# Mamba input tiles of a hybrid decoder step: handed to the scan by blocks, with three fixed tiles

## The chip, the cores and the metric

The kernel runs on one core of a Trainium2 chip. A core has TensorE (PE, matrix products), VectorE (DVE), ScalarE (ACT), GpSimd (POOL) and DMA queues, here driven by SyncE (SP); each works off its own instructions in their written order and waits for the others by semaphores. The metric is the device time of one execution in microseconds, as the median of several runs.

## The reference

One step of a trunk with two layers, for a prompt of 1024 tokens and eight samples of one token each. Layer 0 is a Conformer convolution module, layer 1 a Mamba-2 mixer; each is followed by a SwiGLU network and a small gated embedding. All is float32. The change lies in the Mamba mixer:

```python
zxbcdt = u @ w_in                                   # z 2048, x 2048, B 1024, C 1024, dt 32 columns
xbc, new_conv = causal_dwconv(xbc, conv_buf, w_conv, b_conv)     # 4 taps over the tokens
xbc = jax.nn.silu(xbc)
...
y, final = ssd(xs, dt, A, Bm, Cm, s0)               # 8 groups; 8 chunks of 128 tokens in each
y = y + d_skip * xs
yg = y * jax.nn.silu(z)
yg = yg * lax.rsqrt(jnp.mean(yg * yg, axis=-1, keepdims=True) + EPS)   # within a group
out = (yg * norm_g) @ w_out
```

In `ssd` a chunk's output is the sum of a product within the chunk (`y_diag`: C times B, weighted by decays, times x) and one with the state that the chunks before it left; then the state is decayed and the chunk's own contribution added. The samples take one step of the same recurrence, each from a state of its own.

## The kernel before

Activations are stored with channels on the 128 partitions and tokens along the row. A row has T = 1032 columns, eight phases of 128 prompt tokens and one sample each. Every float32 product is made of three (`mm3`, L130 to L132) of a rounded part `hi` and a rest `lo` of each factor; ScalarE makes `hi` (L110), VectorE `lo` (L111).

**Input tiles.** `in_proj` computes one tile of 128 columns of `u @ w_in`. It goes through the tokens in three blocks (BLKP) of 388, 386 and 258 columns, 24 matmuls each, into one of three PSUM banks with the tag `mm`; `by_token` lets ScalarE evict the bank, in two or three pieces (L843, L848), into the tile in the order of tokens. After a block `tick` counts down the queued transposes (`later`), so that two blocks later the matmul stream takes them up. A generator, `in_proj` yields after each block.

**Raw tiles.** The eviction of an x, B or C tile goes to a raw tile with three zero columns ahead of the tokens for the convolution. `new_raw` takes it from a pool with two places and clears the three columns by a memset on POOL (L815). `xbc_tile` calls it, drives `in_proj` to its end, and then issues the convolution for both halves of the tokens: a product on ScalarE (L980), three multiply-adds on VectorE (L983), silu on ScalarE (L985). Thus a place is free again when its convolution has been done. `z_tile` does the same for z, without a convolution. `to_tokens` transposes a half into tokens by rows (L1005 on TensorE, L1006 on ScalarE).

**Scan.** The order of the input tiles is a list: B, C, x, x, z, z of a group, then the same of the next. The loop over 64 chunks (8 groups of 8) issues in each turn: the decays and the C times B product of the next chunk (`weights_a`), in some turns one whole input tile of the next group, and the chunk's own work (`scale_x`, `chunk`). In a group these turns are those of chunks 0, 1, 3, 4, 5 and 7:

```python
STEPS = (0, 1, 3, 4, 5, 7)
...
elif cc in STEPS:
    step()
```

In `chunk` TensorE makes `ys` (L1093, C with the state before), four `yd` (L1097, within the chunk) and the chunk's contribution to the state (L1109). VectorE makes `yo` (L1102), `yv` (L1099, L1105), `ztok` (L1106) and `state` (L1114 decays it, L1117 adds); ScalarE squares (L1107). After chunk 1 comes `sample`, the samples' step for this group, in four parts: POOL makes two products (L1159, L1160), VectorE an addition (L1161), a product (L1163) and a sum (L1164). The samples' B and C (`bcs`, L1148) go out to memory and come back to all partitions as `bcb` (L1152), a single tile for two of the parts. Where matmuls of one engine stand between others' it is the scheduler's placing; the order on VectorE, ScalarE and POOL is made before the run too.

In group 7 there is no next group: its turns are filled with the first two quarters of the w_out product, whose inputs are loaded into tiles of the same pool (`staging`).

Of the kernel before, what the change touches and what calls it, by code (L numbers as in the profile page):

```python
# [8 lines left out]
F32 = mybir.dt.float32  # L9
F32R = mybir.dt.float32r  # L10
AF = mybir.ActivationFunctionType
# [5 lines left out]
P = 128  # L17
# [4 lines left out]
T = SEQ + NS  # L22
# [35 lines left out]
def trunk_kernel(ctx: ExitStack, tc: tile.TileContext, I, O):  # L58
    nc = tc.nc
    V, S, G, TE = nc.vector, nc.scalar, nc.gpsimd, nc.tensor  # L60
# [85 lines left out]
    def later(k, fn):  # L146
        queue.append([k, fn])
# [83 lines left out]
    def ple_products(pool, ps, i, pt, tag, halves=(0, 1), w=None):  # L231
        for s in halves:
            w = w or kview(slab(I["w_proj"][i, s], 1024), 2)
            for mm in range(4):
                m = 4 * s + mm
                stg = pool.tile([P, T], F32, name="pstg", tag=tag, bufs=3 if tag == "v" else 2)
                for o, n in BLK:
                    a = ps.tile([P, 512], F32, name="a", tag="mm")
                    product(a[:, :n], w, mm * P, pt, o, n)
                    S.activation(out=stg[:, o:o + n], in_=a[:, :n], func=AF.Copy)  # L240
                nc.scalar.dma_start(out=proj_d[i][m], in_=stg)
                yield
            w = None
# [295 lines left out]
    with tc.tile_pool(name="l0", bufs=2, reuse_waits="tile") as pool:  # L539
# [50 lines left out]
        with tc.tile_pool(name="conv", bufs=2, reuse_waits="tile") as cp:  # L590
# [93 lines left out]
            it = pw1(0, vs, w1)  # L684
# [18 lines left out]
            for m in range(KT):  # L703
# [4 lines left out]
                if m == KT - 1:  # L708
# [4 lines left out]
                    it = chain(ple_products(cp, ps, 1, U[6:], "v"), ple_products(cp, ps, 0, U[4:6], "v", (1,)))  # L713
# [52 lines left out]
            for m in range(KT):  # L766
                x, y, z = apply(0, m)
# [6 lines left out]
            for b in (1, 2):  # L774
                finish(b, (y,), (z,))
                for m in range(KT):
                    x, y, z = apply(b, m)
# [4 lines left out]
    for j in range(2):  # L782
# [4 lines left out]
        for m in range(KT):  # L787
            w = kview(slab(I["w_pw2"][m], 1024), KT)
# [21 lines left out]

    l1 = ExitStack()
    pa = l1.enter_context(tc.tile_pool(name="l1a", bufs=1, reuse_waits="tile"))
    def new_raw():
        raw = pa.tile([P, 3 + T], F32, name="raw", tag="raw", bufs=2)
        G.memset(raw[:, 0:3], 0.0)  # L815
        return raw

    raws = [new_raw(), new_raw()]
    cst = pa.tile([P, 32, NS, 4], F32, name="cst")
    ncp = pa.tile([P, 32, 3], F32, name="ncp")  # L820
    xs_all = pa.tile([P, 32, NS], F32, name="xs_all")
    zs_all = pa.tile([P, 16, NS], F32, name="zs_all")
# [28 lines left out]
    def in_proj(w, dst, sample, func, off=0):  # L851
        for o, n in BLKP:
            a = bank("mm", mm_bufs[0])
            product(a[:, :n], w, 0, U, o, n)
            by_token(dst[:, off:off + T], a, o, n, func)
            if o == BLKP[-1][0]:
                G.tensor_copy(out=sample, in_=dst[:, off + SEQ:off + T])
            tick()
            yield
# [16 lines left out]
    with tc.tile_pool(name="ps1", bufs=1, space=PSUM, reuse_waits="tile") as ps, \  # L876
            tc.tile_pool(name="l1b", bufs=2, reuse_waits="tile") as pool:
        mm_bufs[0] = 3
        C9 = 9
        nac = pool.tile([P, 8, NH], F32, name="nac", bufs=1)  # L880
        ea = pool.tile([P, 8, NH], F32, name="ea", bufs=1)
        dtd = pool.tile([P, 8, NH], F32, name="dtd", bufs=1)
# [11 lines left out]
        def decays():  # L894
# [3 lines left out]
            def v9(t, i):  # L898
                return t[:, 288 * i:288 * i + 288].rearrange("p (c h) -> p c h", c=C9)

# [19 lines left out]
            for c in range(8):  # L920
# [18 lines left out]
            V.scalar_tensor_tensor(out=a_t, in0=dt, scalar=-1.0,  # L939
                                   in1=ea_log.unsqueeze(1).broadcast_to([P, C9, NH]), op0=ALU.mult, op1=ALU.mult)  # L940
            a_flat = a_t[:, :8].rearrange("p c h -> p (c h)")
# [27 lines left out]
        def xbc_tile(ct, w, raw=None):  # L969
            if raw is None:  # L970
                raw = new_raw()
                for _ in in_proj(w, raw, cst[:, ct, :, 3], AF.Copy, 3):
                    pass
            G.tensor_copy(out=ncp[:, ct], in_=raw[:, SEQ:SEQ + 3])
            tag = "xf" if ct < 16 else ("bf" if ct < 24 else "cf")
            out = []
            for hf in range(2):
                d = pool.tile([P, 512], F32, name=tag, tag=tag, bufs=2 if ct < 16 else 3)
                o = 512 * hf
                S.activation(out=d, in_=raw[:, 3 + o:515 + o], func=AF.Identity, scale=col("w_conv", 4 * ct + 3),  # L980
                             bias=col("b_conv", ct))
                for j in (2, 1, 0):
                    V.scalar_tensor_tensor(out=d, in0=raw[:, j + o:j + o + 512], scalar=col("w_conv", 4 * ct + j),  # L983
                                           in1=d, op0=ALU.mult, op1=ALU.add)
                S.activation(out=d, in_=d, func=AF.Silu)  # L985
                out.append(d)
            pr = pool.tile([P, NS, 4], F32, name="spr", tag="spr")
            V.tensor_tensor(out=pr, in0=cst[:, ct],
                            in1=col("w_conv", 4 * ct, 4).unsqueeze(1).broadcast_to([P, NS, 4]), op=ALU.mult)
            s8 = pool.tile([P, NS], F32, name="s8", tag="s8")  # L990
            V.tensor_reduce(out=s8, in_=pr, axis=AX.X, op=ALU.add)
            S.activation(out=xs_all[:, ct], in_=s8, func=AF.Silu, bias=col("b_conv", ct))
            return out

        def z_tile(zt, w):
            z = pool.tile([P, T], F32, name="zf", tag="zf", bufs=1)
            for _ in in_proj(w, z, zs_all[:, zt], AF.Silu):
                pass
            return z[:, :512], z[:, 512:SEQ]

# [12 lines left out]
        def xbc_group(g):  # L1013
            d = grp[g]

            def b_():
                d["bf"] = bf = xbc_tile(16 + g, *(weights() if g else (None, raws[0])))
                d["btok"] = []
                for hf in range(2):
                    t = pool.tile([P, 4, P], F32, name="btok", tag="btok", bufs=3)  # L1020
                    later(2, lambda hf=hf, t=t: to_tokens(bf[hf], t, 0))
                    d["btok"].append(t)

            def c_():
                d["cf"] = xbc_tile(24 + g, *(weights() if g else (None, raws[1])))

            def x_(i):
                if i == 0:
                    d["xtok"] = [pool.tile([P, 4, 256], F32, name="xtok", tag="xtok", bufs=3) for _ in range(2)]
                xf = xbc_tile(2 * g + i, *weights())  # L1030
                for hf in range(2):
                    later(2, lambda hf=hf: to_tokens(xf[hf], d["xtok"][hf], i * P))

            return [(32 + g, b_), (40 + g, c_), (16 + 2 * g, lambda: x_(0)), (17 + 2 * g, lambda: x_(1))]

        def z_group(g):
            d = grp[g]

            def z_(i):
                if i == 0:  # L1040
                    d["ztok"] = [pool.tile([P, 4, 256], F32, name="ztok", tag="ztok", bufs=4) for _ in range(2)]
                zf = z_tile(2 * g + i, *weights())
                for hf in range(2):
                    later(2, lambda hf=hf: to_tokens(zf[hf], d["ztok"][hf], i * P))

            return [(2 * g, lambda: z_(0)), (2 * g + 1, lambda: z_(1))]
# [170 lines left out]
        order = xbc_group(0)  # L1217
# [4 lines left out]
        def prefetch(i):  # L1222
            if i < len(order):
                nextw.append(win(order[i][0]))

        def weights():
            return [nextw.pop(0)]

        order[0][1]()
        order[1][1]()  # L1230
        prefetch(2)
        prefetch(3)
        pos = 2

        def step():
            nonlocal pos
            order[pos][1]()
            pos += 1
            prefetch(pos + 1)

        decays()
        step()
# [2 lines left out]

        step()
        step()
        STEPS = (0, 1, 3, 4, 5, 7)

        def first_quarters():  # L1250
            for m in range(KT):
# [3 lines left out]
                yield from w_out(q, load_y(q, U[:4], staging, ysm))  # L1255

        def staging():
            return pa.tile([P, 3 + T], F32, name="yr", tag="raw", bufs=2)

        fill = None  # L1260
        ahead = weights_a(0, 0)
        for i in range(8 * NG):
            g, cc = divmod(i, 8)
            cur, ahead = ahead, weights_a(*divmod(i + 1, 8)) if i + 1 < 8 * NG else None
            if g == NG - 1:
                fill = fill or first_quarters()
                next(fill)
                next(fill)
            elif cc in STEPS:
                step()  # L1270
            if i == 0:
                flush()
            chunk(g, cc, *cur, *scale_x(g, cc))
            if i == 8 * NG - 9:
                nc.sync.dma_start(out=O["sconv_p"], in_=ncp)
                nc.sync.dma_start(out=O["sconv_s"], in_=cst)
                sample(NG - 1)
            if cc == 1 and g < NG - 1:
                sample(g)
            if cc == 4 and g in (5, 7):  # L1280
                sample_norm(*((0, 6) if g == 5 else (6, 8)))
        flush()


    with tc.tile_pool(name="ps2", bufs=7, space=PSUM, reuse_waits="tile") as ps:
        mm_bufs[0] = 7
# [7 lines left out]
        for j in range(2):  # L1294
            for s in range(4):
                w = kview(slab(I["w_out"][3, s], 1024), 4)
# [164 lines left out]
```

## Time and profile before

| | |
|---|---|
| median of 3 runs | 3101.6 us (3101.09 to 3102.29) |
| profiled execution, its time | 3103.0 us |
| its span on the core | 3101.2 us |
| granted TensorE clock, mean share of full speed | 0.975 |
| TensorE busy | 2941.5 us (95%) |
| VectorE busy | 2022.4 us (65%) |
| ScalarE busy | 1402.5 us (45%) |
| POOL busy | 556.8 us (18%) |

The scan of groups 0 to 6 lies at about 1230 to 2010 us of the span, group 7 behind it until 2147. A busy share is an average over stages of different kinds: what a change is worth is read from the waits of the stage that it touches.

### The profile page before, as it was taken

The page shows a single profiled execution, that of the slowest core. Times are in us where ns is not written, and L with a number is a line of the kernel's source. Part 1 is how long each engine was busy: PE and PEld are TensorE (multiplying, and loading weights), DVE is VectorE, ACT ScalarE, POOL GpSimd, SP SyncE. Part 2 cuts the span into 40 slices and gives each one's busy share as a digit, 9 for nine tenths or more (in the row PEclk, how much of TensorE's full clock was granted, in tenths as well). Part 3 has the DMA queues.
Part 4 walks back from the last instruction along what each step waited for, and adds up shares of the span by engine and source line. Part 5 has one row for each costly group of instructions (what it writes and reads, how often), then busy time and mean ns, then how long its engine had stood idle before and what let it go on. Part 6 is the DMA issues. An engine that isn't in the chain of part 4 may idle for free. (4 is left out here: it accounts for less than half of the span.)

```text
span 3101.2 us, 51140 instructions
## 1 busy us (share of the span) xinstructions
PE 2941.5 (95%) x20513; PEld 2893.8 (93%) x20513; DVE 2022.4 (65%) x3255; ACT 1402.5 (45%) x2470; POOL 556.8 (18%) x571
## 2 busy tenths in 40 slices
PE   9997989999999999999999999988979999989997
PEld 9997889999999999899999999888979999989997
DVE  8778695555444488467788777875595555444486
ACT  6225453333321155667667676732353333321164
POOL 0003210000000021144454444441210000000022
PEclk9998999999999999999999999998999999999998
DMA  6335522222252233122233222442422222252222
GB/s 191 75 80 179 160 88 94 76 79 73 82 185 89 65 111 102 54 87 91 92 108 106 94 92 100 144 159 79 124 77 82 81 83 83 69 179 88 65 88 87
DMA packets 146415, 313.23 MB, mean 101 GB/s; under 512 B 16513, under 2 KB 66049, under 8 KB 146177
## 3 DMA queue, kind: packets, MB, share of 16 engines
q1 hardware_dynamic: 143872, 301.51, 30.0%
q10 hardware_dynamic: 2304, 8.46, 0.7%
q8 instruction: 161, 2.64, 0.4%
q14 instruction: 78, 0.63, 0.1%
HBM read 233.15 MB, written 68.35 MB: 97 GB/s over the span
## 5 line engine op out<-in xcount | busy, mean ns | idle before, releaser
L130 PE MATMUL mm<-u,whi 128*128 128x388 f32 (+3 forms) x1472 | 481.1, 328 | 35.0 <-ACT raw L848 25.2
L131 PE MATMUL mm<-u,whi 128*128 128x388 f32 (+3 forms) x1472 | 487.3, 331 | 7.6 <-DVE u L111 7.6
L132 PE MATMUL mm<-u,wlo 128*128 128x388 f32 (+3 forms) x1472 | 477.7, 325 | 0.6 <-DVE wlo L111 0.6
L110 ACT ACTIVATE whi<-wraw 128x1024 fp32r<-128x1024 f32 (+1 forms) x199 | 207.8, 1044 | 454.4 <-PE a L131 263.7
L130 PEld LDWEIGHTS mm<-u,whi 128*128 128x128 f32 x1472 | 283.3, 193 | 39.2 <-ACT raw L848 26.6
L130 PE MATMUL a<-hh,whi 128*128 128x344 f32 x984 | 309.0, 321 | 10.9 <-ACT hh L110 10.9
L131 PE MATMUL a<-hh,whi 128*128 128x344 f32 x984 | 315.3, 321 | 0.6 <-DVE hh L111 0.6
L132 PE MATMUL a<-hh,wlo 128*128 128x344 f32 x984 | 314.5, 320 | 0.0
L195 POOL TENSOR_TENSOR stat<-stat,sq 128x344 f32<-128x344 f32 x56 | 60.0, 1072 | 1392.7 <-ACT sq L194 1390.4
L131 PEld LDWEIGHTS mm<-u,whi 128*128 128x128 f32 x1472 | 283.9, 193 | 12.4 <-DVE u L111 10.3
L132 PEld LDWEIGHTS mm<-u,wlo 128*128 128x128 f32 x1472 | 283.6, 193 | 2.5 <-DVE wlo L111 0.8
L111 DVE TENSOR_TENSOR wlo<-wraw,whi 128x1024 fp32r<-128x1024 f32 (+1 forms) x199 | 244.3, 1228 | 62.5 <-ACT whi L110 59.2
L460 DVE TENSOR_TENSOR h<-a,h 128x344 f32<-128x344 f32 x288 | 144.7, 512 | 174.9 <-PE a L132 174.1
L130 PE MATMUL a<-u,whi 128*128 128x344 f32 (+1 forms) x712 | 224.9, 317 | 15.4 <-DVE u L751 9.8
L131 PE MATMUL a<-u,whi 128*128 128x344 f32 (+1 forms) x712 | 223.2, 315 | 7.2 <-DVE u L752 7.2
L132 PE MATMUL a<-u,wlo 128*128 128x344 f32 (+1 forms) x712 | 220.9, 313 | 2.7 <-DVE wlo L111 2.7
L130 PEld LDWEIGHTS a<-hh,whi 128*128 128x128 f32 x984 | 184.4, 189 | 11.4 <-ACT hh L110 11.4
L131 PEld LDWEIGHTS a<-hh,whi 128*128 128x128 f32 x984 | 185.5, 189 | 1.0 <-DVE hh L111 1.0
L132 PEld LDWEIGHTS a<-hh,wlo 128*128 128x128 f32 x984 | 185.4, 189 | 0.0
L130 PEld LDWEIGHTS a<-u,whi 128*128 128x128 f32 x712 | 137.3, 193 | 18.3 <-DVE u L751 10.9
L111 DVE TENSOR_TENSOR wal<-sa,wah 128x1024 fp32r<-128x1024 f32 x44 | 53.9, 1224 | 151.6 <-ACT wah L110 151.6
L131 PEld LDWEIGHTS a<-u,whi 128*128 128x128 f32 x712 | 137.1, 193 | 10.0 <-DVE u L752 8.7
(361 smaller groups left out, 8652.6 us busy)
## 6 DMA issues: line engine op xcount, KB each, us to landing
wraw<-in_w_in SPq DMA_DIRECT2D x48, 512.0 KB, 3.7
hid<-hid SPq DMA_DIRECT2D x88, 258.0 KB, 2.5
hraw<-hid SPq DMA_DIRECT2D x44, 516.0 KB, 4.2
wraw<-in_w_gate SPq DMA_DIRECT2D x44, 512.0 KB, 3.2
wraw<-in_w_up SPq DMA_DIRECT2D x44, 512.0 KB, 3.3
wraw<-in_w_pw SPq DMA_DIRECT2D x32, 512.0 KB, 3.4
wraw<-in_w_down SPq DMA_DIRECT2D x32, 512.0 KB, 3.4
am<-ac_d SPq DMA_DIRECT2D x64, 256.0 KB, 3.3
```

The costliest lines, as they stand in the source:

```text
L110: S.activation(out=hi, in_=raw, func=AF.Copy)
L111: eng.tensor_tensor(out=lo, in0=raw, in1=as32(hi), op=ALU.subtract)
L130: TE.matmul(out, lhsT=wh, rhs=xh, start=start, stop=False, skip_group_check=onto)
L131: TE.matmul(out, lhsT=wh, rhs=xl, start=False, stop=False, skip_group_check=onto)
L132: TE.matmul(out, lhsT=wl, rhs=xh, start=False, stop=stop, skip_group_check=onto)
L195: return eng.tensor_tensor(out=self.acc[:, o:o + n], in0=self.acc[:, o:o + n], in1=sq[:, :n], op=ALU.add)
L460: V.tensor_tensor(out=h[m][:, o:o + n], in0=a[:, :n], in1=h[m][:, o:o + n], op=ALU.add)
```

## The change

Three things change. The raw tiles are no longer taken from a pool and cleared at each use, but are two fixed tiles, cleared once, and handed out in turn (`ring`); a third one, `raw2`, is added for the time of the scan and taken out again behind it. It serves as a third staging tile in group 7 too. The input tiles are no longer issued whole: `xbc_tile` and `z_tile` yield after the first two blocks, and the loop takes as many blocks in each turn as BLOCKS says, 18 in a group as before, two or three in each of the eight turns.

```diff
--- before.py
+++ after.py
@@ -810,10 +810,13 @@
 
     l1 = ExitStack()
     pa = l1.enter_context(tc.tile_pool(name="l1a", bufs=1, reuse_waits="tile"))
+    ring = [pa.tile([P, 3 + T], F32, name=f"raw{i}") for i in range(2)]
+    for raw in ring:
+        G.memset(raw[:, 0:3], 0.0)
+
     def new_raw():
-        raw = pa.tile([P, 3 + T], F32, name="raw", tag="raw", bufs=2)
-        G.memset(raw[:, 0:3], 0.0)
-        return raw
+        ring.append(ring.pop(0))
+        return ring[-1]
 
     raws = [new_raw(), new_raw()]
     cst = pa.tile([P, 32, NS, 4], F32, name="cst")
@@ -877,6 +880,8 @@
             tc.tile_pool(name="l1b", bufs=2, reuse_waits="tile") as pool:
         mm_bufs[0] = 3
         C9 = 9
+        raw2 = pool.tile([P, 3 + T], F32, name="raw2", bufs=1)
+        G.memset(raw2[:, 0:3], 0.0)
         nac = pool.tile([P, 8, NH], F32, name="nac", bufs=1)
         ea = pool.tile([P, 8, NH], F32, name="ea", bufs=1)
         dtd = pool.tile([P, 8, NH], F32, name="dtd", bufs=1)
@@ -969,7 +974,11 @@
         def xbc_tile(ct, w, raw=None):
             if raw is None:
                 raw = new_raw()
-                for _ in in_proj(w, raw, cst[:, ct, :, 3], AF.Copy, 3):
+                it = in_proj(w, raw, cst[:, ct, :, 3], AF.Copy, 3)
+                for _ in range(2):
+                    next(it)
+                    yield
+                for _ in it:
                     pass
             G.tensor_copy(out=ncp[:, ct], in_=raw[:, SEQ:SEQ + 3])
             tag = "xf" if ct < 16 else ("bf" if ct < 24 else "cf")
@@ -994,7 +1003,11 @@
 
         def z_tile(zt, w):
             z = pool.tile([P, T], F32, name="zf", tag="zf", bufs=1)
-            for _ in in_proj(w, z, zs_all[:, zt], AF.Silu):
+            it = in_proj(w, z, zs_all[:, zt], AF.Silu)
+            for _ in range(2):
+                next(it)
+                yield
+            for _ in it:
                 pass
             return z[:, :512], z[:, 512:SEQ]
 
@@ -1014,7 +1027,7 @@
             d = grp[g]
 
             def b_():
-                d["bf"] = bf = xbc_tile(16 + g, *(weights() if g else (None, raws[0])))
+                d["bf"] = bf = yield from xbc_tile(16 + g, *(weights() if g else (None, raws[0])))
                 d["btok"] = []
                 for hf in range(2):
                     t = pool.tile([P, 4, P], F32, name="btok", tag="btok", bufs=3)
@@ -1022,12 +1035,12 @@
                     d["btok"].append(t)
 
...
@@ -1226,17 +1239,26 @@
         def weights():
             return [nextw.pop(0)]
 
-        order[0][1]()
-        order[1][1]()
+        for i in range(2):
+            for _ in order[i][1]():
+                pass
+        ring.insert(0, raw2)
         prefetch(2)
         prefetch(3)
-        pos = 2
+
+        def blocks():
+
+            for pos in range(2, len(order)):
+                for _ in order[pos][1]():
+                    yield
+                prefetch(pos + 2)
+                yield
+
+        block = blocks()
 
         def step():
-            nonlocal pos
-            order[pos][1]()
-            pos += 1
-            prefetch(pos + 1)
+            for _ in range(3):
+                next(block)
 
         decays()
         step()
@@ -1245,7 +1267,7 @@
 
         step()
         step()
-        STEPS = (0, 1, 3, 4, 5, 7)
+        BLOCKS = (2, 2, 3, 2, 2, 2, 3, 2)
 
         def first_quarters():
             for m in range(KT):
@@ -1255,7 +1277,7 @@
                 yield from w_out(q, load_y(q, U[:4], staging, ysm))
 
         def staging():
-            return pa.tile([P, 3 + T], F32, name="yr", tag="raw", bufs=2)
+            return new_raw()
 
         fill = None
         ahead = weights_a(0, 0)
@@ -1266,8 +1288,9 @@
                 fill = fill or first_quarters()
                 next(fill)
                 next(fill)
-            elif cc in STEPS:
-                step()
+            else:
+                for _ in range(BLOCKS[cc]):
+                    next(block)
             if i == 0:
                 flush()
             chunk(g, cc, *cur, *scale_x(g, cc))
@@ -1281,6 +1304,7 @@
                 sample_norm(*((0, 6) if g == 5 else (6, 8)))
         flush()
 
+    ring[:] = [r for r in ring if r is not raw2]
 
     with tc.tile_pool(name="ps2", bufs=7, space=PSUM, reuse_waits="tile") as ps:
         mm_bufs[0] = 7
```

The hunk left out makes the same change in `c_`, `x_` and `z_` as that shown in `b_`: `yield from` in front of the call. In the changed kernel the lines of the scan have numbers that are higher by 9 to 13: L815 is L884 for the new tile, L843 and L848 are L846 and L851, L980, L983, L985 and L992 are L989, L992, L994 and L1001, and from L1005 on 13 are added (L1093 is L1106, L1163 is L1176).

The rows that follow are parts of the order in which instructions stand on an engine, all from group 1, behind its chunk 1. On VectorE, the second of the sample's four parts ends with its reading of `bcb` (L1163); the next part begins with the addition to `s0_16302` (L1161). Before, 15 instructions stand between the two, of which the last eleven are shown here, with that addition at the end:

```order
L1073 TENSOR_TENSOR xd_16795<-xtok_15319,dt_11974 128x256
L1064 TENSOR_TENSOR cbm_16517<-cb_16515,umask_142 128x128
L988 TENSOR_TENSOR spr_16468<-cst_11968,vec_140 128x32
L983 SCALAR_TENSOR_TENSOR cf_16231<-raw_16129,vec_140,cf_16231 128x512
L983 SCALAR_TENSOR_TENSOR xf_16456<-raw_16372,vec_140,xf_16456 128x512
L983 SCALAR_TENSOR_TENSOR xf_16462<-raw_16372,vec_140,xf_16462 128x512
L1105 TENSOR_TENSOR yv_16487<-yv_16487,yo_16494 128x256
L991 TENSOR_REDUCE s8_16470<-spr_16468 128x8
L983 SCALAR_TENSOR_TENSOR cf_16231<-raw_16129,vec_140,cf_16231 128x512
L1117 TENSOR_TENSOR state_16500<-state_16500,ys_16486 128x256
L1075 TENSOR_TENSOR xdd_16797<-xtok_15319,dtd_13185 128x256
L1161 TENSOR_TENSOR s0_16302<-s0_16302,xb_16304 128x512
```

In the changed kernel the same two (L1176, then L1174 with `s0_16190`) stand six instructions apart:

```order
L1176 TENSOR_TENSOR xb_16181<-s0_16179,bcb_16168 128x512
L1118 TENSOR_TENSOR yv_16348<-yv_16348,yo_16355 128x256
L1177 TENSOR_REDUCE ysm_11972<-xb_16181 128x4
L1119 TENSOR_TENSOR ztok_15623<-yv_16348,ztok_15623 128x256
L1130 TENSOR_TENSOR state_16361<-state_16361,ys_16347 128x256
L1088 TENSOR_TENSOR xdd_16580<-xtok_15268,dtd_13187 128x256
L1127 TENSOR_TENSOR state_16476<-state_16361,cd_13188 128x256
L1174 TENSOR_TENSOR s0_16190<-s0_16190,xb_16192 128x512
```

The multiply-adds of C's and x's convolution that stood between the two parts now stand elsewhere, most of them behind the third. On ScalarE, from `bcs` of the sample (L1148) to the silu of the second half of B (L985, `bf_16077`), before:

```order
L1148 ACTIVATE bcs_16275<-cb_16274 8x256
L992 ACT_TABLE_LOAD
L992 ACTIVATE xs_all_11970<-s8_16239,vec_140 128x8
L1107 ACTIVATE yv_16256,ssq_16102<-ztok_15641 128x256
L985 ACTIVATE cf_16225<-cf_16225 128x512
L980 ACTIVATE bf_16077<-raw_15959,vec_140 128x512
L1059 ACT_TABLE_LOAD
L1059 ACTIVATE L_16360<-am_16357,nac_13183 128x128 x4
L985 ACT_TABLE_LOAD
L985 ACTIVATE bf_16077<-bf_16077 128x512
```

The same stretch of the changed kernel, from L1161 to L994 with `bf_16090`:

```order
L1161 ACTIVATE bcs_16163<-cb_16162 8x256
L1120 ACTIVATE yv_16144,ssq_16029<-ztok_15623 128x256
L851 ACTIVATE raw1_11965<-mm_16221 128x128
L846 ACTIVATE raw1_11965<-mm_16221 128x2x129
L989 ACTIVATE bf_16090<-raw0_11964,vec_140 128x512
L1019 ACTIVATE btok_16101<-tp_16248 128x512
L110 ACTIVATE whi_16306<-wraw_16305 128x1024
L846 ACTIVATE raw1_11965<-mm_16260 128x2x129
L994 ACT_TABLE_LOAD
L994 ACTIVATE bf_16090<-bf_16090 128x512
```

The eviction of C's second block (L851, L846 into `raw1`) now stands ahead of the first product of B's second half (L989); before, C's tile had been evicted whole ahead of this place. On TensorE, the transposes of the first half of the second x tile (L1005, `tp<-ident,xf`) before, with `ys` and `yd` of a chunk ahead of and between them and the first block of the z tile behind them:

```order
L130 MATMUL mm<-u,whi 128x258
L131 MATMUL mm<-u,whi 128x258
L132 MATMUL mm<-u,wlo 128x258
L1093 MATMUL ys<-state,cf 128x256
L1097 MATMUL yd<-xd,L 128x128 x2
L1005 MATMUL tp<-ident,xf 128x128 x4
L1097 MATMUL yd<-xd,L 128x128
L1005 MATMUL tp<-ident,xf 128x128 x4
L1097 MATMUL yd<-xd,L 128x128
L1062 MATMUL cb<-cf,bf 128x128
L130 MATMUL mm<-u,whi 128x388
```

And the same transposes (L1018) in the changed kernel:

```order
L132 MATMUL mm<-u,wlo 128x258
L130 MATMUL mm<-u,whi 128x258
L1018 MATMUL tp<-ident,xf 128x128
L1122 MATMUL ys<-xdd,btok 128x256
L1018 MATMUL tp<-ident,xf 128x128 x3
L131 MATMUL mm<-u,whi 128x258
L132 MATMUL mm<-u,wlo 128x258
L130 MATMUL mm<-u,whi 128x258
L1018 MATMUL tp<-ident,xf 128x128 x4
L131 MATMUL mm<-u,whi 128x258
L132 MATMUL mm<-u,wlo 128x258
```

The transposes stand in the middle of a block of 258 columns now, with the state's product (`ys<-xdd,btok`) between them.

## Rows read from the trace of the kernel before

**Rows 1.** Waits of TensorE, 1290 to 2010 us: total, times, longest.
```profile
PE mm L130 <- ACT raw L848: 25.2, 7, 3.9
PE ys L1093 <- DVE state L1117: 7.0, 7, 1.0
PE tp L1005 <- ACT xf L985: 5.0, 5, 2.2
```

**Rows 2.** Windows of low clock; columns as in rows 3; the last row their sum.
```profile
1487.50:1490.80 3.30, 3.30 (x12) 3.30 (x11) 3.30 (x7) 3.27 (x7) 3.30 (x3) 0.50 0.27 78
...
sum 26.70, PE 24.93 PEld 24.93 DVE 26.70 ACT 25.98 POOL 20.90; mean PE 4.15 PEld 4.16 DVE 4.45 ACT 4.33 POOL 3.48
```

**Rows 3.** Windows: us, busy us (instructions) of each engine, PEclk, DMA share, GB/s.
```profile
1437.84:1535.94 98.10, 92.69 (x603) 90.68 (x602) 75.01 (x126) 67.39 (x132) 47.45 (x48) 0.98 0.30 99
...
1450.37:1503.37 53.00, 47.59 (x301) 46.04 (x300) 52.56 (x82) 38.56 (x73) 30.36 (x31) 0.97 0.36 120
...
1503.37:1547.84 44.47, 44.47 (x301) 44.07 (x299) 22.53 (x42) 28.28 (x59) 16.90 (x17) 1.00 0.23 75
...
2011.70:2147.30 135.60, 120.25 (x712) 114.82 (x712) 93.73 (x155) 44.44 (x73) 39.99 (x37) 0.92 0.38 128
```

**Rows 4.** TensorE's timeline, group 1: start us, duration us, instruction [idle before <-releaser].
```profile
1442.16 0.33 PE L130 MATMUL mm<-u,whi 128*128 128x386 f32 x1
...
1446.41 0.28 PE L130 MATMUL mm<-u,whi 128*128 128x258 f32 x1
...
1447.37 0.60 PE L1005 MATMUL tp<-ident,bf 128*128 128x128 f32 x4
...
1449.73 0.59 PE L1093 MATMUL ys<-state,cf 128*128 128x256 f32 x2
...
1450.16 1.05 PE L1097 MATMUL yd<-xd,L 128*128 128x128 f32 x8
...
1467.10 0.70 PE L1093 MATMUL ys<-state,cf 128*128 128x256 f32 x2 [0.99 <-DVE state L1117]
...
1486.09 0.45 PE L130 MATMUL mm<-u,whi 128*128 128x388 f32 x1 [3.63 <-ACT raw L848]
...
1503.09 0.66 PE L1005 MATMUL tp<-ident,xf 128*128 128x128 f32 x4 [0.79 <-ACT xf L985]
```

**Rows 5.** ScalarE's timeline, group 1.
```profile
1465.12 0.50 ACT L848 ACTIVATE raw<-mm 128x1 f32<-128x1 f32 x2
...
1465.95 0.42 ACT L1107 ACTIVATE yv<-ztok 128x256 f32<-128x256 f32 x1
...
1467.84 0.81 ACT L980 ACTIVATE cf<-raw,vec 128x512 f32<-128x512 f32 x1
...
1483.97 0.42 ACT L1107 ACTIVATE yv<-ztok 128x256 f32<-128x256 f32 x1 [4.97 <-DVE ztok L1106]
```

**Rows 6.** POOL's timeline at the memset, group 1.
```profile
1484.66 0.10 POOL L815 MEMSET raw<- 128x3 f32 x1 [3.27 <-DVE cf L983]
```

**Rows 7.** VectorE's timeline, group 1.
```profile
1469.95 1.41 DVE L1163 TENSOR_TENSOR xb<-s,bcb 128x512 f32<-128x512 f32 x1
...
1481.60 0.68 DVE L1161 TENSOR_TENSOR s<-s,xb 128x512 f32<-128x512 f32 x1
...
1505.82 0.42 DVE L1099 TENSOR_TENSOR yv<-yd,xs 128x256 f32<-128x256 f32 x1
...
1508.37 0.42 DVE L1114 TENSOR_TENSOR state<-state,cd 128x256 f32<-128x256 f32 x1
```

**Rows 8.** Timelines of SyncE's DMA queue and of POOL, group 1.
```profile
1471.44 0.32 SPq L1152 DMA_DIRECT2D bcb<-bc_d  x1
...
1475.35 1.49 POOL L1159 TENSOR_TENSOR xb<-bcb,xdt 128x512 f32<-128x512 f32 x1 [0.79 <-DMA bcb<-bc_d]
```

**Rows 9.** Tiles bf and xf, 1290 to 2010 us: L983, ns min/median/max.
```profile
L983 DVE SCALAR_TENSOR_TENSOR bf<-raw,vec,bf x42: 734/1445/1843, 1343.2 to 1953.0; 128x512 f32<-128x512 f32 x42
...
L983 DVE SCALAR_TENSOR_TENSOR xf<-raw,vec,xf x90: 732/740/1830, 1303.1 to 1992.8; 128x512 f32<-128x512 f32 x90
```

More of the change, by code (lines that the diff above doesn't have):

```diff
@@ L1024, in c_ @@
             def c_():
-                d["cf"] = xbc_tile(24 + g, *(weights() if g else (None, raws[1])))
+                d["cf"] = yield from xbc_tile(24 + g, *(weights() if g else (None, raws[1])))
             def x_(i):
@@ L1029, in x_ @@
                     d["xtok"] = [pool.tile([P, 4, 256], F32, name="xtok", tag="xtok", bufs=3) for _ in range(2)]
-                xf = xbc_tile(2 * g + i, *weights())
+                xf = yield from xbc_tile(2 * g + i, *weights())
                 for hf in range(2):
@@ L1041, in z_ @@
                     d["ztok"] = [pool.tile([P, 4, 256], F32, name="ztok", tag="ztok", bufs=4) for _ in range(2)]
-                zf = z_tile(2 * g + i, *weights())
+                zf = yield from z_tile(2 * g + i, *weights())
                 for hf in range(2):
```

## The prediction

> **What bounds the kernel now.** The change works in the scan, so I first read TensorE's waits in the stretch that holds groups 0 to 6 [rows 1]. Three waits carry all of it that counts: seven times, once in a group, the first matmul of a 388-column block waits for an eviction (L848) to free a bank, 25.2 us; seven waits of the `ys` product for the state, 7.0; five of the transposes for a convolved x tile, 5.0. That is 37.2 us, 5.3 a group. The windows of low clock come next [rows 2]: behind these stalls the granted clock is 0.50, the 1.2 GHz level, for 26.70 us in all; half of that is lost, 13.4 us or 1.9 a group. So some 7.2 us of a group's 98.1 [rows 3] are not matmul work at full speed, about 50 us in seven groups. That is all that a change of order can win here; the remaining time TensorE is busy.
>
> Then I followed one group (1). On TensorE's timeline [rows 4] the `ys` product of chunk 1 starts at 1449.73 and the transposes of the second x tile at 1503.09. I call these 53.36 us the stretch S. All its waits lie in it: 0.99 + 3.63 + 0.79 = 5.41, and 1.65 of half clock (half of the 3.30 us at 1487.50 in [rows 2]); 53.36 - 5.41 - 1.65 = 46.3 us is its matmul work. Beside S, the windows show VectorE busy 52.56 of 53.00 us, and 22.53 of 44.47 in the rest of the group, where TensorE has no gap and clock 1.00 [rows 3]. So S ends when VectorE has done its rows, and TensorE, with 7 us too little to do, waits somewhere in it. Where it waits is told by ScalarE's timeline [rows 5]: the eviction that TensorE wants at 1482.5 stands behind L1107, which waited 4.97 us for VectorE and ran at 1483.97; the matmul follows at 1486.09. The memset of the raw tile waits for VectorE's convolution as well [rows 6], for the same reason: two tiles only.
>
> **The change part by part.** *Memsets.* Each tile's memset takes 0.10 us of POOL [rows 6]; 29 go. POOL is busy 30.36 of S's 53.00 us [rows 3], so 0.10 is hidden by its idle time; bare, it would be 2.9 us in all. I take 0. *Third tile.* An x tile's first block need not wait until C's convolution is done. With the hand-out by blocks this removes the 3.63 us stall of S at its place. It does not remove what VectorE has to do before the second x tile can be transposed.
>
> *Hand-out.* The number of matmuls stays; S gets more of them. Counted from the two orders between the ends of S: 24 more of 386 columns, seven more of 258, two more `yd` and four more transposes. 24 of 386 columns took 4.25 us (1442.16 to 1446.41), eight of 258 took 0.96 (to 1447.37), so seven 0.84; four transposes 0.44 and two `yd` 0.45 as they stand between others (bounds: 0.26 as a quarter of 1.05, 0.60 for the four) [rows 4]. Sum 6.0; S's matmul work becomes 52.3 us and the rest of the group loses 6.0 from its 44.5. If S keeps its length, TensorE's loss falls from 7.1 to 1.1.
>
> *VectorE in S.* I count 80 rows before, 82 after, ahead of the same finish; priced form by form by their mean durations 49.7 and 49.8 us: equal. But its rows now stand closer to what they wait for, in two places.
> (a) The second half of B's convolution needs ScalarE's first product, which in the new order stands behind the eviction of C's second block. TensorE ends that block 0.43 (`ys`) + 0.9 (`yd`, 1.05 long with its end under the next) + 4.25 (24 matmuls) + 0.43 (the state's `ys`) + 0.3 (the end of the last matmul and the step to ScalarE, an estimate) = 6.3 us after the `ys` of chunk 1; the eviction's pieces took 0.83 (1465.12 to 1465.95), the product 0.81 [rows 5]: 8.0 us. VectorE stands there after the wait of 0.64 for `ys` and nine rows. At the stretch's mean, 52.56/82 = 0.64 a row, that is 6.4; at the price of the eight rows from 1505.82 to 1508.79, 0.37 each [rows 7], 4.0. They are nearly all of the latter kind, so I take 4.8: a hole of 3.2 us (1.6 to 4.0).
> (b) The third step of the sample's state waits for `bcb`, a single tile, loaded again once the second step has read it. The issue at 1471.44 led to POOL's product at 1475.35, which took 1.49: 5.4 us to its end [rows 8]. Before, VectorE had from 1471.36 to 1481.60 for other things [rows 7]; now six rows, 3.4 us (2.2 at 0.37, 3.8 at 0.64): a hole of 2.0 (1.6 to 3.2).
> Together 5.2 (3.2 to 7.2), and nothing else is ready on that queue, which runs in its written order: what waits behind are C's and x's convolutions, and so the end of S. S becomes 58.6 us (56.6 to 60.6). The loss in it is 58.6 - 52.3 = 6.3.
>
> *Second half of x.* The second half's transposes stand behind the finish of that half; two more VectorE rows there, 0.6 us. *Clock.* The stalls go to other places, and the low clock stays behind some; where VectorE sets S's end a half-speed TensorE costs nothing, so 0.3 of it falls after S. Sum of a group: 6.3 + 0.6 + 0.3 = 7.2 against 7.2 before; net 0, bounds -2.0 and +2.0 from the holes: seven groups, 0 (-14 to +14).
>
> *Tail.* Three staging tiles for the first w_out quarters instead of two. TensorE is busy 120.25 of 135.60 us in group 7, at clock 0.92 [rows 3]; a third load and split no longer waits. Its gain lies between 0 and that idle 15.4; as the other 13 us have other causes, I take 2.
>
> Sum: the profiled execution 3103.0 us (span 3101.2 and 1.8 around it) + 0 - 2 = 3101; it lies 1.4 above the median of the runs shown, 3101.6, so on that scale **3099**.
>
> **A rule that speaks on the memsets and on VectorE's price.** [rows 9] show what a convolution row costs: the same L983 takes 734 to 1843 ns on B and 732 to 1830 on x. The Trainium skill, page "SBUF — State Buffer", section "Who interferes with whom", says that a VectorE instruction with two SBUF inputs is blocked by a GpSimd instruction that reads SBUF, and not by one that only writes it; so by it the removed memsets give VectorE nothing and the tensor products of POOL are the price. The two-level durations agree. By the rule as by the row the memsets' term is 0.
>
> **Rivals.**
> A, the forecast: the wait moves from the eviction to x's transposes. For it: VectorE is full in S before and has nothing less to do [rows 3]. 3092 to 3105, likeliest 3099.
> B, the holes don't arise. Then S stays 53.4 and the loss in it is 1.1 + 0.6 instead of 7.1: 5.4 a group, 38 us, 3062; half of the holes gives 3080. For it: the rows of VectorE may be slow where I took them fast, so that the eviction and the sample's load are in time. Against it: the distances above, 3.4 us for a path of 5.4.
> C, slower: VectorE's rows get dearer by meeting POOL. The order puts other rows beside POOL's products; a row of L983 is 740 or 1445 ns by the medians of x and B [rows 9]. 21 of them stand in S; three that change from 0.74 to 1.44 cost 2.1 us a group, 15 us: 3114. From +0.9 a group it decides. For it: the third tile lets x's convolution start while POOL makes the sample's products; against it: the counter case is as open (all at 0.74 would give 4.7 a group back).
> By that rule of the Trainium skill (page "SBUF — State Buffer", same section) it decides between A and C which convolution lies beside POOL's reading rows; no row of before tells.
> D: the change does as good as nothing, since only the place of the work moves and its sum doesn't; that ends in A's range.
>
> **How the numbers follow.** A and D 0.43, B in some degree 0.33, C 0.24. 0.2%, 6.2 us, is what a measurement of this kernel tells from no change: faster is below 3095.4, slower above 3107.8. A gives faster 0.10, same 0.31, slower 0.02; B faster 0.31, same 0.02; C same 0.02, slower 0.22. Sum 0.41, 0.35, 0.24. The range takes A, the half of B (3080) and C to its price: 3077 to 3114 leaves out the full B and a dearer C, about 2 in 10. The likeliest case's own range is 3092 to 3105.
>
> **What would show it.** Right: TensorE's wait for the eviction falls from 25.2 to under 3 us; its wait of the transposes for x rises from 5.0 to 20 to 35; S is 57 to 60 us; VectorE waits some 3 us a group for B's first product, or for that chunk's `ys`, and 2 us for POOL's sample product, seven times each; the low clock stays behind three to seven stalls. Wrong: S near 53 us and waits below 15 in all (B); S above 61 with VectorE busy throughout and L983's mean up (C); a TensorE wait in the part of the group after S, which I have without any.

## The result, and the profile after

The changed kernel takes 3126.95 us (median of 4 runs, 3124.76 to 3130.78), the kernel before 3101.35 beside it. The ratio is 1.0085, with a 95% interval of 1.007 to 1.010: 25.6 us slower, where no change was forecast and 3114 was the range's end. The profiled execution has a span of 3129.0 us.

The first part of the page (busy us, share, instructions) against the table of before: TensorE runs as many instructions, VectorE as many, POOL 29 fewer, and ScalarE 28 more.

```profile
PE 2949.5 (94%) x20513; PEld 2900.7 (93%) x20513; DVE 2009.3 (64%) x3255; ACT 1441.5 (46%) x2498; POOL 548.5 (18%) x542
```

TensorE's waits in the scan, the view of [rows 1]:

```profile
PE tp L1018 <- ACT xf L994: 28.3, 9, 4.5
PE ys L1106 <- DVE state L1130: 26.2, 14, 2.8
PE ys L1122 <- DVE yo L1115: 2.7, 3, 1.5
```

The wait for the eviction is gone, as forecast. The transposes of x wait 28.3 us, within the 20 to 35 that were forecast (28.7 to 2040 us, where the changed kernel's group 6 ends). The products of `ys` wait 26.2 us for the state, which was not. The three rows make 57.2 us where those of [rows 1] make 37.2.

Windows over group 1, from the `ys` of chunk 1 to the first x tile's transposes, from there to the second's, and from there to the next group's chunk 1 (columns as in [rows 3]); as fourth row the second of these windows in group 2; and two rows of TensorE's timeline in group 1, a wait in the first window and the one that ends it:

```profile
1446.13:1497.07 50.94, 43.80 (x274) 42.30 (x273) 45.00 (x69) 36.05 (x65) 27.48 (x24) 0.96 0.34 111
1497.07:1510.09 13.02, 13.02 (x69) 12.75 (x70) 11.02 (x20) 12.00 (x23) 5.35 (x6) 0.78 0.32 102
1510.09:1548.60 38.51, 38.51 (x261) 38.07 (x260) 18.02 (x36) 25.25 (x50) 14.85 (x15) 1.00 0.23 70
...
1599.94:1612.40 12.46, 10.79 (x69) 10.10 (x70) 10.95 (x20) 11.49 (x22) 5.21 (x5) 1.00 0.28 96
```

```profile
1485.28 0.70 PE L1106 MATMUL ys<-state,cf 128*128 128x256 f32 x2 [2.81 <-DVE state L1130]
...
1497.07 1.97 PE L1018 MATMUL tp<-ident,xf 128*128 128x128 f32 x8 [2.89 <-ACT xf L994]
```

S is 1446.13 to 1510.09, 63.96 us; 58.6 was forecast. The part behind it is 38.51 us at clock 1.00 without a gap, as forecast (44.5 less 6.0). In S TensorE stands idle for 50.94 - 43.80 = 7.14 us, and loses 2.0 us more by a clock of 0.96 in the first window and 2.9 by 0.78 in the second: 12.0 us, where 6.9 was forecast for idle time and clock together (6.3 and 0.6). The low clock is not what makes the group long: in group 2 the second window has clock 1.00 and TensorE stands idle in it for 1.67 us instead (12.46 less 10.79), and that group takes 102.37 us where group 1 takes 102.47. The second x tile's transposes, which were to be the place where TensorE waits last, wait for nothing in group 1 and 1.54 us in group 2; the first tile's wait 2.89 and 2.87 us.

What they wait for stands on ScalarE. First VectorE's timeline, then ScalarE's, before 1497.07:

```profile
1484.82 0.41 DVE L1130 TENSOR_TENSOR state<-state,ys 128x256 f32<-128x256 f32 x1
...
1490.00 0.74 DVE L992 SCALAR_TENSOR_TENSOR xf<-raw,vec,xf 128x512 f32<-128x512 f32 x1
...
1498.51 2.22 DVE L111 TENSOR_TENSOR wlo<-wraw,whi 128x1024 fp32r<-128x1024 f32 x1 [3.30 <-ACT whi L110]
```

```profile
1484.93 0.30 ACT L1001 ACTIVATE xs_all<-s,vec 128x8 f32<-128x8 f32 x1 [4.63 <-DVE s L1000]
1487.86 0.42 ACT L1120 ACTIVATE yv<-ztok 128x256 f32<-128x256 f32 x1 [2.62 <-DVE ztok L1119]
...
1489.15 1.28 ACT L1072 ACT_TABLE_LOAD   x1
1490.45 0.99 ACT L1072 ACTIVATE L<-am,nac 128x128 f32<-128x128 f32 x3
1491.44 1.28 ACT L994 ACT_TABLE_LOAD   x1
1492.74 0.63 ACT L994 ACTIVATE cf<-cf 128x512 f32<-128x512 f32 x1
1493.37 1.28 ACT L1072 ACT_TABLE_LOAD   x1
1494.67 0.40 ACT L1072 ACTIVATE L<-am,nac 128x128 f32<-128x128 f32 x1
1495.09 1.28 ACT L994 ACT_TABLE_LOAD   x1
1496.38 1.15 ACT L994 ACTIVATE xf<-xf 128x512 f32<-128x512 f32 x2
```

VectorE has ended the first half of x at 1490.00 + 0.74 = 1490.74 us. The silu of it (L994, `xf<-xf`) runs at 1496.38. In the 5.6 us between, ScalarE goes to and fro between the exps of chunk 5's decays and silus, and loads its function table at 1489.15, 1491.44, 1493.37 and 1495.09, 1.28 us each. A silu had run at 1484.93 (L1001), without a load since: had x's silus come next, they would have needed none. VectorE comes to a stop as well: its row at 1498.51 waits 3.30 us for ScalarE. The wait for the state is VectorE's own: its rows followed each other without a wait from 1472.92 on, it added the state (L1130) at 1484.82, and the `ys` that needs it followed at 1485.28. Over the whole program the rows of table loads of the scan's lines are, after and then before:

```profile
L1072 ACT ACT_TABLE_LOAD x57 | 73.1, 1283 | 26.9 <-issue 26.3
...
L994 ACT ACT_TABLE_LOAD x36 | 46.2, 1283 | 0.6
...
L1001 ACT ACT_TABLE_LOAD x17 | 21.8, 1283 | 0.3
...
L846 ACT ACT_TABLE_LOAD x7 | 9.0, 1283 | 0.0
```

```profile
L1059 ACT ACT_TABLE_LOAD x43 | 55.2, 1283 | 0.8
...
L992 ACT ACT_TABLE_LOAD x24 | 30.8, 1283 | 0.3
...
L843 ACT ACT_TABLE_LOAD x14 | 18.0, 1283 | 0.2
...
L985 ACT ACT_TABLE_LOAD x8 | 10.3, 1283 | 0.1
```

117 against 89: 28 more, four in each of the seven groups. They are the 28 instructions of the first row above, 36 us of ScalarE.

### The profile page after: what moved, and what is told of

It is laid out like the page before. It is cut to its first block, busy times and chain, and to the rows that moved or that the text cites. A ratio compares the mean times of both kernels' runs of the same rounds, so it can differ in the third digit from the quotient of the medians.

```text
span 3129.0 us, 51102 instructions
## 1 busy us (share of the span) xinstructions
PE 2949.5 (94%) x20513; PEld 2900.7 (93%) x20513; DVE 2009.3 (64%) x3255; ACT 1441.5 (46%) x2498; POOL 548.5 (18%) x542
## 5 line engine op out<-in xcount | busy, mean ns | idle before, releaser
L111 DVE TENSOR_TENSOR wlo<-wraw,whi 128x1024 fp32r<-128x1024 f32 (+1 forms) x199 | 252.3, 1268 | 113.0 <-ACT whi L110 109.7
```

The costliest lines, as they stand in the source:

```text
L111: eng.tensor_tensor(out=lo, in0=raw, in1=as32(hi), op=ALU.subtract)
```

## The experiments

Theory 1 was that VectorE's rows ahead of the first x tile make the waits, theory 2 that the third tile does; theory 3, that ScalarE's table loads do, came with the rows above, after the first four runs. Each time is a median of 4 or more runs; the ratio, with its 95% interval, is to the kernel before, timed beside it.

**Tiles alone, blocks alone.** The first keeps the three fixed tiles and the old turns:

```diff
-                for _ in range(BLOCKS[cc]):
-                    next(block)
+            elif cc in STEPS:
+                step()
```

> The three fixed tiles, whole tiles handed out in the turns of chunks 0, 1, 3, 4, 5 and 7 as before the change. Theory 1 (the hand-out by blocks costs: it puts 43.9 us of VectorE's rows ahead of the first x tile's transposes where 36.7 stood, TensorE waits there and runs on at the low clock): 3092 to 3106 us, the wait for the eviction of about 25 us gone or moved to the x tiles' transposes. Theory 2 (the third tile costs: x's convolution starts earlier and takes VectorE and ScalarE from the chunks' chain): 3115 to 3130.

It takes 3113.5 us, ratio 1.0044 (1.0029 to 1.0059): between the theories, and with as many table loads as before. Windows of S and of the part behind it in group 1, of the part behind it in group 3, and the wait:

```profile
1449.68:1503.04 53.36, 46.80 (x302) 44.61 (x300) 51.54 (x82) 39.33 (x73) 29.73 (x27) 0.99 0.36 119
1503.04:1550.66 47.62, 47.62 (x301) 47.11 (x301) 23.80 (x43) 28.59 (x59) 17.33 (x17) 0.94 0.23 70
...
1704.14:1750.32 46.18, 46.18 (x301) 45.79 (x301) 23.37 (x43) 28.58 (x59) 17.84 (x17) 0.97 0.21 72
```

```profile
PE tp L1018 <- ACT xf L994: 35.6, 14, 4.0
```

S is 53.36 us in group 1, what it was before the change. The wait for the eviction has been taken away and has come back, whole, at the transposes of x, most of it at those that end S, as the prediction said of the third tile. So VectorE does set S's length when whole tiles are handed out. What is new lies behind S: 47.62 and 46.18 us where [rows 3] have 44.47 at clock 1.00, since the low clock, which stood inside S after the eviction's wait, now stands behind its end (0.94 and 0.97). 6% and 3% of these are 2.9 and 1.4 us a group. A third tile that removes a wait is so paid for by the place where the wait comes again.

The second hands out blocks, from two tiles of the pool, cleared each time:

```diff
-    ring = [pa.tile([P, 3 + T], F32, name=f"raw{i}") for i in range(2)]
...
+        raw = pa.tile([P, 3 + T], F32, name="raw", tag="raw", bufs=2)
+        G.memset(raw[:, 0:3], 0.0)
```

> Blocks handed out as in the change, but two tiles from the pool, cleared at each use. Theory 1: 3122 to 3145 us, the changed kernel's waits with the old wait for an eviction on top. Theory 2: 3092 to 3108.

3129.5 us, ratio 1.0095 (1.0080 to 1.0110). ScalarE's instructions are 2498 here too. The old wait for the eviction is back, 20.0 us; the wait of the transposes is smaller for it, that for the state is not:

```profile
PE ys L1101 <- DVE state L1125: 26.0, 18, 2.8
PE mm L130 <- ACT raw L848: 20.0, 7, 3.7
PE tp L1013 <- ACT xf L989: 8.4, 7, 1.6
```

The hand-out by blocks brings the loss by itself; beside it the third tile neither adds to the loss nor heals it, though with whole tiles it costs 12 us.

**The samples' step later.** In the changed kernel and in the one before, `sample(g)` is called after chunk 5, where VectorE has room (busy 22.53 of 44.47 us behind S in [rows 3]):

```diff
-            if cc == 1 and g < NG - 1:
+            if cc == 5 and g < NG - 1:
                 sample(g)
```

> The changed kernel with the samples' step called after chunk 5 instead of chunk 1 (and the norm of the first six groups' samples two chunks later): it takes 12 rows, 9.1 us, and the sample's load out of VectorE's queue ahead of the first x tile. Theory 1: TensorE's waits in the scan fall from 57 to under 20 us and the low clock with them, 3045 to 3080 us. Theory 2: VectorE's rows are not the cause, above 3105.

> The kernel before with the same move of the samples' step. Theory 1: VectorE was full up to the second x tile here too; of the 7.2 us lost in a group some 5 come back, 3052 to 3080 us. Theory 2: no change beyond 10 us, 3090 to 3105.

3077.4 us (0.9926, 0.9912 to 0.9941) and 3082.7 (0.9939, 0.9922 to 0.9956). The second lies just above theory 1's range: 18.5 us came back where some 35 were expected, with as many table loads as before, so VectorE's rows were a bound in the kernel before. For the changed kernel the first doesn't tell theory 1 from theory 3: ScalarE's page row has 2471 instructions in it, so 27 table loads went with the rows. The three rows of waits that made 57.2 us make 16.5 in its scan, as expected.

**Silus first.** One order is added on ScalarE; no work changes but the table loads. `e` is an exp of the decays, `silu_x[0]` the last silu of the first x tile:

```diff
+                if cc == 5 and g < NG - 1:
+                    behind(e, silu_x[0])
```

> The changed kernel with one more order on ScalarE: the exps of chunk 5's decays stand behind the silus of the first x tile. In the changed kernel's trace ScalarE loads its table four times between 1489 and 1497 us, as exps and silus alternate; VectorE had ended the first half of that x tile at 1490.74 and its silu ran at 1496.38. With this order the program has 28 table loads fewer, as many as the kernel before. Theory 3 (ScalarE's alternation is what holds up the first x tile): the wait of the transposes falls from 28 to under 10 us, the low clock with it, 3085 to 3110 us. Theory 1 (VectorE's rows hold it up): 3116 to 3130.

3096.7 us: 30 us less than the changed kernel, and a ratio of 0.9979 (0.9970 to 0.9988) to the one before. The table loads are 89 again. TensorE's waits, the windows of group 1 cut at the same places, and ScalarE around the first x tile:

```profile
PE ys L1112 <- DVE state L1136: 12.7, 12, 1.9
PE ys L1128 <- DVE yo L1121: 11.5, 10, 1.3
PE tp L1022 <- ACT xf L996: 8.1, 6, 1.4
PE yd L1116 <- POOL L L1084: 5.9, 7, 1.0
```

```profile
1443.28:1487.50 44.22, 41.67 (x271) 40.17 (x270) 38.90 (x64) 25.89 (x50) 20.86 (x20) 1.00 0.36 119
1487.50:1504.17 16.67, 13.02 (x82) 11.87 (x82) 15.99 (x27) 16.46 (x31) 9.73 (x10) 1.00 0.31 95
1504.17:1541.43 37.26, 37.26 (x251) 36.92 (x251) 19.34 (x37) 25.37 (x51) 15.67 (x15) 1.00 0.23 76
```

```profile
1486.81 1.36 ACT L996 ACTIVATE xf<-xf 128x512 f32<-128x512 f32 x2 [1.37 <-DVE xf L994]
1488.19 1.28 ACT L1076 ACT_TABLE_LOAD   x1
```

The silu of the first half runs at 1486.81 and the load stands behind it; the wait of the transposes falls from 28.3 to 8.1 us, that for the state from 26.2 to 12.7, and the clock is 1.00 in all three windows. Other waits grow (`yo` 11.5, `yd` 5.9): all of TensorE's waits in the scan make 41.0 us here, 60.1 in the changed kernel and 40.3 before. VectorE's rows up to the end of the first half of x are the same 60 in the same order, so theory 1 alone does not hold.

The order moves one thing besides the loads: two of POOL's products of the decays (L1078, L1069) come later too. In the changed kernel they run from 1480.44 to 1483.86, and beside them VectorE's x row (1480.95) and `yv` row (1482.66) take 1.78 and 1.48 us; with the silus first the same two rows take 0.74 and 0.41, and POOL stands idle. VectorE so ends the first half of x 43.5 us behind the `ys` of chunk 1 instead of 44.6: 1.1 of the 6.7 us by which its silu comes earlier (43.5 instead of 50.3).

**The loads given back.** To this kernel, four table loads ahead of the same silu, by activations of one element whose results nothing uses:

```diff
+                    mark = S.activation(out=tiny[:, :1], in_=tiny[:, 1:], func=AF.Exp)
+                    behind(mark, silu_x[2])
+                    for f in (AF.Silu, AF.Exp):
+                        last, mark = mark, S.activation(out=tiny[:, :1], in_=tiny[:, 1:], func=f)
+                        behind(mark, last)
...
+                    behind(silu, mark)
```

> The kernel with the silus first (3096.7 us), to which ScalarE's four table loads ahead of the first x tile's silu are given back by three one-element activations (exp, silu, exp) between the silu of C and that of x, in six of the groups; they compute nothing that is used. Theory 3 (the loads, 1.28 us each, are the price): the transposes wait 4 to 5 us a group again and the low clock returns, 3118 to 3135 us. Rival (that the exps of chunk 5 come later is what helped, not the loads): 3092 to 3104.

3123.8 us, ratio 1.0065 (1.0050 to 1.0080): 27 us more for six groups, 4.5 each. Three of the four loads on ScalarE's timeline in group 1, and the waits, for x's silu 35.1 us where it was 8.1, for the state 13.3 where it was 12.7:

```profile
1484.12 1.28 ACT L1002 ACT_TABLE_LOAD   x1
...
1485.63 1.28 ACT L1002 ACT_TABLE_LOAD   x1
...
1487.15 1.28 ACT L1004 ACT_TABLE_LOAD   x1
1488.44 1.15 ACT L1004 ACTIVATE xf<-xf 128x512 f32<-128x512 f32 x2
```

```profile
PE tp L1034 <- ACT xf L1004: 35.1, 12, 4.6
PE ys L1124 <- DVE state L1148: 13.3, 14, 2.0
```

Group 0 was left without them, and is a control in the same execution: from its `ys` of chunk 1 to group 1's it takes 98.15 us, from group 1's to group 2's 102.36 (starts 1342.34, 1440.49 and 1542.85 on TensorE's timeline). So the loads in that place are the price, whichever exps bring them. The wait for the state did not come back with them, and yet the group is as long as the changed kernel's 102.47 us: that wait, half of which went with the order of the exps and not with the loads, was covered by the one for x's silu that follows it, as far as these lengths show.

**A filled wait.** 16 matmuls more in a group, written into the bank that the transposes then overwrite; the scheduler put them in front of chunk 4's `ys`:

```diff
+            for _ in range(fill):
+                TE.matmul(b[:, :388], lhsT=U[0][0][:, :P], rhs=U[0][0][:, :388], start=True, stop=True)
```

> The changed kernel with 16 matmuls of 388 columns more in a group (2.8 us of TensorE, seven times; their result is overwritten by the transposes), which stand in the order just ahead of chunk 4's ys, where TensorE waited 2.8 us for the state. If a wait is followed by the low clock and costs that on top, they take the wait's place and the time falls by the clock's part, 3108 to 3124 us. If the low clock doesn't come from this wait: 3124 to 3132; if there was no wait to fill, 20 us more, 3147.

3127.9 us, ratio 1.0081 (1.0064 to 1.0097), against 3126.95 without them, with 20 us of TensorE's work more:

```profile
PE tp L1020 <- ACT xf L994: 31.5, 12, 3.4
PE ys L1108 <- DVE state L1132: 8.0, 12, 2.3
```

They took the place of the wait for the state (26.2 to 8.0 us); the other stays. But this order also has 14 table loads fewer (2484 instructions), two in each group. At the price of the run before, 4.5 us for four, they could give some 16 us back (an estimate), so the run shows neither what the filled wait was worth nor what the clock's part is.

**Transposes a block later.** `later(2, ...)` of the x tiles becomes `later(3, ...)`.

> The changed kernel with the transposes of the x tiles one block later (three blocks behind the tile's issue instead of two, some 3 to 4 us of TensorE's work). Theories 1 and 3: the wait at the first x tile goes, 28 us to under 12, 3098 to 3118 us. Rival: the second x tile's convolution then waits for the tile that the first gives back and the wait comes again there, 3120 to 3135.

3123.7 us, ratio 1.0056 (1.0036 to 1.0076). The first tile's transposes stayed where they were, at 51.0 us behind the `ys` of chunk 1 in group 1 (50.9 in the changed kernel), and the wait is 24.0 us; only the second tile's moved. The run tests nothing of the theories.

**Towards a better kernel.** Whole tiles from three fixed tiles, the samples' step after chunk 5:

> The three fixed tiles with whole tiles handed out, and the samples' step after chunk 5. With the pool's two tiles the same move gave 3082.7. If the third tile hurts only because VectorE is full there, it costs nothing now: 3072 to 3084 us. If it costs by itself (12 us without the move): 3090 to 3098.

3082.5 us (0.9927, 0.9912 to 0.9942), beside 3082.7 with the pool's two tiles: the third tile costs nothing once VectorE has room in S. Then the samples' step in two halves, after chunks 5 and 7, once with blocks and silus first, once with whole tiles:

> The silus first and the samples' step in two halves, after chunk 5 and after chunk 7, where VectorE has room. Both causes are away: waits in the scan under 20 us, 3062 to 3080 us; if the late samples' step is limited by its own loads and by POOL, not better than 3077.

> Whole tiles handed out from three fixed tiles, with the samples' step in the same two halves. If the hand-out by blocks is worth something once both causes are away, this is slower than the run with blocks beside it, 3075 to 3088 us; if not, the same as that, within 5 us.

3073.7 us (0.9899, 0.9882 to 0.9915) and 3071.3 (0.9895, 0.9880 to 0.9910). Both beat the kernel before by some 30 us and are equal within their intervals; the hand-out by blocks is worth nothing there. All of TensorE's waits in the scan still make 34 us in each of the two. The largest of them with whole tiles:

```profile
PE tp L1145 <- DVE ztok L1139: 16.4, 7, 2.9
```

## Why the prediction was wrong

**The step that failed** is the sentence "So S ends when VectorE has done its rows", carried over to the changed kernel. It holds for whole tiles: in the run of tiles alone S keeps its 53.36 us. With blocks it doesn't, because another engine's queue became longer: the hand-out by blocks puts exps between silus on ScalarE and adds 28 table loads, for which the sum had no term. In group 1 the first x tile's silu runs 5.6 us after VectorE has done its half, and the group takes 102.5 us where 98.1 was forecast to stay. ScalarE was looked at only where an eviction or a product stood in its queue; the stretch of its order ahead of the prediction has three loads before and one after, and so pointed the other way. Removed, the loads give 30 us back (with them went the 1.1 us of VectorE's time in group 1); given back to six groups, they cost 27. That is as much as the 25.6 us, and gives the sign.

**The Trainium skill states the rule**, on the page "ScalarE: Activation LUTs", section "Table sets: the hidden batching unit": call the functions of one table set together and then those of the next, since a change of set loads the table. The trace agrees, with 1283 ns for each load in the rows above. The rule speaks against this change, and was not weighed.

**The clock's term** was 0.3 us a group behind S's end and none inside it. Inside S that was right in kind: group 1 of the changed kernel loses 4.9 us there and group 2 some 1.5 (clock 0.97 and 1.00), and both are as long, since another engine sets the end. Behind S it was mis-sized for whole tiles, where the tiles alone lose 1.4 to 2.9: their waits had moved to the place that ends the bound stretch, and what follows there is TensorE's own time.

**The holes in VectorE's queue** came at their places, but smaller. VectorE's waits in the changed kernel, the samples' addition and the convolution of B:

```profile
DVE s L1174 <- POOL xb L1172: 10.8, 10, 1.9
...
DVE bf L992 <- ACT bf L989: 5.2, 7, 0.8
```

That is 1.5 and 0.7 us a group where 2.0 and 3.2 were forecast: their sum of 5.2 was 3 us too high. With the silus first S is 60.9 us (1443.28 to 1504.17) and the group 98.15, against 98.1 before. That is the net nothing of the forecast, and 3096.7 us lies by its 3099; but S did not get its length from the holes as forecast, so this is in part luck. The forecast's last sum is off by a little too: 3101 less 1.4 is 3099.6, and nothing hangs on it.

**Matmul work**: forecast 52.3 us for S and 38.5 for what follows; measured 51.9 (63.96 less 7.1 and 4.9) and 38.51. **Memsets**: 0, and no run speaks against it; they can't be seen apart. **Tail**: from the `ys` of chunk 1 in group 7 to the end 1078.6 us before (2022.56 on), 1075.0 after (2053.98 on): 3.6 us gained, 2 forecast. In the run of blocks alone, with two staging tiles, it is 1078.2 (2050.39 to 3128.6), so the gain goes with the third.

**Rivals.** C, dearer rows on VectorE, ended on the right side for a wrong reason. Its sign, VectorE busy throughout S, did not come: it is busy 45.00 + 11.02 of the 63.96 us. The convolution's rows of x up to 2040 us (count, busy us, mean ns), before and then after:

```profile
L983 DVE SCALAR_TENSOR_TENSOR xf<-raw,vec,xf 128x512 f32<-128x512 f32 x90 | 75.1, 873 | 0.4 <-ACT xf L980 0.4
...
L992 DVE SCALAR_TENSOR_TENSOR xf<-raw,vec,xf 128x512 f32<-128x512 f32 x90 | 85.3, 964 | 0.4 <-ACT xf L989 0.4
```

x's rows got dearer in the mean, B's and C's cheaper (1251 to 1117 and 898 to 816 ns): 165.4 us for all three before, 166.5 after. VectorE's busy time in the whole program fell from 2022.4 to 2009.3 us. B, no holes, came half true, and its gain didn't: ScalarE stood in the place of VectorE.

## What to carry to other kernels

When a change interleaves work in smaller pieces, count what each engine's queue gains in instructions, ScalarE's table loads first: alternation of exp and silu is work that the diff of this change doesn't show. A wait that is removed while another engine bounds the stretch comes back at the stretch's end, and there the low clock behind it is no longer covered. And look for the work that can leave the bound stretch: here the samples' step, a few lines, was worth more than the tiles and the blocks.

## What the runs showed of the hardware

The price of a VectorE row moves between kernels with no change in its operands: the convolution's x rows took 873 ns in the mean before and 964 after, B's 1251 and 1117. Single rows lie between 0.73 and 1.84 us [rows 9], so a median can mislead: B's went from 1445 to 752 ns while its mean fell by a tenth. In group 1 the same two rows took 1.78 and 1.48 us beside POOL's products and 0.74 and 0.41 without them; no run tried POOL's products by themselves.

A change between exp and silu on ScalarE cost one load of 1283 ns, and the next activation began 1.30 us after the one before had ended (1489.15 to 1490.45). A square between two silus brought no load (1483.14 in the run of silus first).

The same low clock cost nearly nothing where another engine set the end of the stretch (102.47 us at a clock of 0.95, 102.37 at 0.98, groups 1 and 2 of the changed kernel), and its full share behind that end (47.62 us at 0.94 instead of 44.47 at 1.00, in the run of tiles alone).
